# Shared access of VectorE and Pool counted as one queue in the planner, three places of a fused layer reordered

## The chip, the cores and the metric

The kernel runs on one core of a Trainium2 chip. The metric is the device time of one execution in microseconds (us). The engines are named as in the profile: PE (TensorE matmul, PEld its weight load), DVE (VectorE), ACT (ScalarE), POOL (GpSimd) and SP (SyncE, which issues all DMAs here). A matmul result lies in PSUM, which has eight banks; POOL instructions in this program never touch PSUM.

## What is computed

One layer over 1024 latent tokens and 256 context tokens, width 1024, in fp32 accuracy. Cut to what matters:

```python
pl = project(modulate(x, sh_x, sc_x), w_in)       # 11 streams out of one projection
pc = project(modulate(ctx, sh_c, sc_c), w_in)
s_f, s_b = final states of the context            # gated linear attention (GLA)
o_gla = bidir_gla(q, k, v, la_f, la_b, s_f, s_b)  # 4 heads, chunks of 64, two directions
q1, q2, k1, k2, dv = diff_streams(...)            # 8 heads: RMS norm, gains, rotary positions
...
a = softmax(s1) - lam * softmax(s2)               # differential attention over 1280 keys
o_diff = a @ v
a = rms_norm(o_gla) * gla_gain * silu(gla_gate)
b = rms_norm(o_diff) * diff_gain * silu(diff_gate)
y = sigmoid(m_gla) * (a @ w_br_gla) + sigmoid(m_diff) * (b @ w_br_diff)
return x + g_x * (y @ w_out)
```

## The kernel before

Every large product is made of three matmuls (`mm3`): an operand is split into a rounded high part `hi` and a rest `lo`, and hi·hi, hi·lo and lo·hi are added up in one PSUM bank. A split costs one copy that rounds (on ACT, or on POOL from SBUF) and one subtraction (on DVE or POOL).

Instructions of PE, ACT, DVE and POOL stand in the order in which a planner, `Driver` (L58), emits them. The program is a set of Python generators. Each yields the time at which it wants to go on; `Driver.op` (L96) keeps a clock of each engine (`free`), adds a cost to it for each instruction (given by `Engine.emit`, L189) and notes when a tile is ready, `LAT` after the end. The generator that is due earliest, by priority, emits next. On the chip each engine then works through its own list in that order and waits by semaphores. `either` (L374) takes DVE or POOL for a subtraction, by whose clock gives the earlier end.

The stages, in the order of time: the modulated input `h` (to about 100 us); the plain projection jobs of `stream` (L889), under which the first half of the GLA runs (`gla_a`, L1450: decays, factors, scores); then `sevens` (L1090), four projections (28 products instead of 32, in the manner of Strassen) whose input sums `sums7` (L925) makes on DVE, POOL and ACT out of `h` in tiles `p`, split into tiles `s7`. Its operand "s2" is written over half of `h`, which the plain jobs still read: `before` therefore stores the sum to DRAM (`d_s2`) and loads it back after the plain jobs. `weights7` (L988) loads and combines the weights for it (tiles `ra`, `rb`, `raw`, split into `w`). Next the last plain jobs (`second`: two tiles of gates, and the query projection `dq`), under which the second half of the GLA runs (`gla_b`, L1653; banks `gs`, `go`, `gt`). A `dq` tile goes through `post_qk` (L1367): ACT copies it to a tile `p` and squares it, DVE sums the squares, POOL raises them to -1/2 and scales the tile, then PE transposes it (`tp`) and the store `d_qT` follows.

Then attention: 64 units (8 heads by 8 query tiles). PE makes scores `s` in banks s0, s1, st; DVE takes maxima (`att_max`); ACT the exponentials `e5`; DVE mixes both (`att_mix`); PE transposes the result in 128-key blocks into one of two banks `b1` (`att_tr`, L1977), 4 + 4 + 2 blocks, where the two tails of a pair of units share one bank; `split2` (L2059) lets ACT copy the bank to a tile `ac` (two of them), and POOL rounds it and subtracts (`at`); PE multiplies with the values (`att_av`). Where attention leaves PE free, a filler runs, `fill` (L2135): the remaining gates, and the two branch products, half a tile (24 matmuls) at a time in a bank `mb`, held back by `pace`; what is left of it runs behind attention, in banks `mc`. Its weights `wt` are split by ACT and DVE (`conv`, L2153). Last comes the output projection.

Memory is handed on in pools that are opened and closed like a stack from the left or the right side (`POOLS`, L247). `mb` lies in pool `psW`, opened on the left by `to_b` when all plain jobs are through; the GLA's banks are pool `psA1`, on the right, closed by `to_gla` when the GLA is through (`ev_b2`).

Of the kernel before, what the change touches and what calls it, by code (L numbers as in the profile page):

```python
# [19 lines left out]
P = 128  # L20
# [36 lines left out]
class Driver:  # L57
# [9 lines left out]
    LAT = dict(PE=0.24, ACT=0.15, DVE=0.15, POOL=0.15)  # L67
# [3 lines left out]
    def __init__(self):  # L71
        self.now = 0.0
        self.free = dict(ACT=0.0, DVE=0.0, POOL=0.0, DGE=0.0, DMA=0.0)
        self.ready, self.last = {}, {}
        self.seq = 0
        self.due, self.future, self.blocked = [], [], 0
# [19 lines left out]
    def op(self, eng, cost, outs, ins):  # L96
# [3 lines left out]
        for x in ins:  # L100
            t = max(t, self.ready.get(self.key(x), 0.0))
# [4 lines left out]
        for x in outs:  # L106
            if eng != "PE":
                t = max(t, self.ready.get(self.key(x), 0.0))
        end = t + cost
        if eng == "PE":  # L110
            self.now = end
        else:
            self.free[eng] = end
# [4 lines left out]
        end += self.LAT[eng]  # L118
        for x in outs:
            self.ready[self.key(x)] = max(end, self.ready.get(self.key(x), 0.0))  # L120
        return At(end)
# [58 lines left out]
class Engine:  # L180
# [5 lines left out]
    def __getattr__(self, what):  # L186
        f = getattr(self.eng, what)

        def emit(out, *args, **kw):  # L189
# [23 lines left out]
            return self.d.op(self.name, c, outs, ins)  # L213
# [8 lines left out]
class Hybrid:  # L222
# [26 lines left out]
                 psA="left", psW="left", psB="left", psC="left", psA1="right", psB1="right", psD="right")  # L249
# [124 lines left out]
    def either(self, out, a, b, op):  # L374

        n = out.free_size()
        dve = self.d.free["DVE"] + 0.16 + 0.00104 * n <= self.d.free["POOL"] + 0.18 + 0.00216 * n
        return (self.dve if dve else self.pool).tensor_tensor(out, a, b, op)

    EDGE = 96  # L380


    def build(self):
        tc = self.tc
        with (
# [4 lines left out]
            with tc.manual_schedule(engines={ENG.PE, ENG.Activation, ENG.DVE, ENG.Pool}):  # L390
# [8 lines left out]
                self.close("psC", "psW", "psD", "sbW", "sbC", "sb", "sbE")  # L399
# [525 lines left out]
    def sums7(self):  # L925
# [7 lines left out]
        ev_s2 = [Event() for _ in range(4)]  # L933
        self.ev_op = {(o, k): Event() for o in self.ORDER[:7] for k in range(4)}
# [10 lines left out]
        for k in range(4):  # L945
# [13 lines left out]
            self.store([(self.d_s2[k], v["11"])], ev=ev_s2[k])  # L959
# [10 lines left out]
        for k in range(4):  # L970
# [17 lines left out]
    def weights7(self, groups):  # L988
# [96 lines left out]
        d.spawn(load(), prio=3)  # L1085
        d.spawn(sums(), prio=3)
        d.spawn(run(), prio=3)
# [119 lines left out]
    def to_gla(self):  # L1207
# [10 lines left out]
        self.open("sbW", "sbB2", "psB1")  # L1218
# [148 lines left out]
    def post_qk(self, isk, c, i, pm, tg):  # L1367
# [45 lines left out]
        e = self.pool.tensor_tensor(r, r, ss.unsqueeze(2).to_broadcast([P, 8, 64]), ALU.mult)  # L1413
# [640 lines left out]
    def att_split(self, g, pt, hi, lo, evs, tag):  # L2054
        e = yield from self.split2(pt, hi, lo, tag, g in self.SG)
# [3 lines left out]
    def split2(self, pt, hi, lo, tag, pool):  # L2059
# [13 lines left out]
        self.rel("ac", e)  # L2073
        return e
# [60 lines left out]
    def fill(self):  # L2135
# [32 lines left out]
        yield self.ev_b  # L2168
# [68 lines left out]
        while n < len(todo):  # L2237
# [8 lines left out]
            for half in range(2):  # L2246
                for x in two:
                    yield pace(i)
# [328 lines left out]
```

## Time and profile before

| what | value |
|---|---|
| three runs | 1728.13, 1728.68 and 1729.07 us, median 1728.68 |
| the profiled execution | 1727.89 us, its span 1726.2 us |
| mean granted TensorE clock | 0.986 of full |
| busy shares of the span | PE 95%, PEld 79%, DVE 68%, POOL 53%, ACT 47% |
| chain that ended last, by engine | PE 75%, POOL 9%, DVE 7%, issue 4%, ACT 3%, DMA 2% |
| DMA | 300.79 MB, mean 174 GB/s |

An execution is 1.7 us longer than its span. In the rows of the profile a line is mostly that of a helper (L190 for all DVE, ACT and POOL instructions, L329 for matmuls, L355 for transposes), so rows are told apart by tiles: `mm<-h,w` reads "tile mm, made from tiles h and w". A matmul's own duration is longer than its distance to the next one, since they overlap.

### The profile page before, as it was taken

What the parts mean: (1) busy time and instruction counts of PE and PEld (TensorE: products, weight loads), DVE (VectorE), ACT (ScalarE), POOL (GpSimd) and SP (SyncE); (2) the same over time, 40 slices, a digit from 0 to 9 for tenths busy, and PEclk for the clock granted to TensorE, in tenths of its full rate; (3) what the DMA queues carried; (4) which work ended last, traced back from release to release, by engine and by line L of the source; (5) the groups of instructions that cost most, each with busy time, mean ns of one, the idle gap of its engine ahead of it and who ended that gap; (6) DMA issues with size and microseconds to landing.
All of it is one profiled execution on the core that took longest, in us unless ns stands there. A gap on an engine that the chain in (4) does not pass through costs nothing.

```text
span 1726.2 us, 24883 instructions
## 1 busy us (share of the span) xinstructions
PE 1646.2 (95%) x8381; PEld 1362.3 (79%) x8381; DVE 1175.0 (68%) x1876; ACT 804.2 (47%) x1606; POOL 920.9 (53%) x908
## 2 busy tenths in 40 slices
PE   8899999999899999999999798999999998899999
PEld 3687788888788888888888587888878787787887
DVE  4764986875624366767686488788887887625694
ACT  4684655643332344343233366566665655511231
POOL 1500886785523245656566448788887888820000
PEclk9999999999999999999999899999999999999999
DMA  8636565544434474459999724335477434259421
GB/s 303 194 138 221 157 208 189 163 127 139 129 117 151 152 239 149 145 181 283 298 313 296 219 72 122 107 112 145 111 228 239 126 116 123 80 196 353 156 99 73
DMA packets 268688, 300.79 MB, mean 174 GB/s; under 512 B 23784, under 2 KB 186512, under 8 KB 268560
## 3 DMA queue, kind: packets, MB, share of 16 engines
q1 hardware_dynamic: 268560, 299.20, 55.5%
q8 instruction: 66, 1.08, 0.3%
q14 instruction: 62, 0.51, 0.1%
HBM read 197.94 MB, written 101.19 MB: 173 GB/s over the span
## 4 chain that ended last, share of the span: by engine, by line
PE 75%; POOL 9%; DVE 7%; issue 4%; ACT 3%; DMA 2%; SPq 0%; ACTq 0%; POOLq 0%; DVEq 0%
PE mm L329 21%; PE mc L329 10%; PE ma L329 10%; POOL at L190 6%; PE gs L329 5%; PE mb L329 5%; PE s L329 5%; PE b L329 4%; PE go L329 4%; PE gt L329 3%; PE tp L329 2%; DVE sm L190 2%; PE b L355 2%; PE tp L355 2%; DMA w<-in_w_ada 1%
## 5 line engine op out<-in xcount | busy, mean ns | idle before, releaser
L190 POOL TENSOR_TENSOR at<-ac,at 128x512 fp32r<-128x512 f32 x160 | 233.2, 1457 | 13.4
L190 DVE TENSOR_REDUCE sm<-s 128x1 f32<-128x1024 f32 (+1 forms) x192 | 197.5, 1040 | 42.5 <-PE s L329 38.4
L329 PE MATMUL mm<-w,h 128*128 128x512 f32 x864 | 219.2, 402 | 6.0 <-DVE us L190 6.0
L190 ACT ACTIVATE e<-s,sm 128x1280 f32<-128x1280 f32 x128 | 169.8, 1330 | 77.1 <-DVE sm L190 63.5
L329 PEld LDWEIGHTS mm<-w,h 128*128 128x128 f32 x864 | 162.1, 191 | 39.5 <-DVE us L190 6.6
L190 POOL TENSOR_SCALAR at<-ac 128x512 fp32r<-128x512 f32 x160 | 136.1, 851 | 95.2 <-ACT ac L190 90.0
L329 PE MATMUL s<-kk,aq 128*128 128x512 f32 (+1 forms) x768 | 174.7, 363 | 6.8 <-ACT e L190 6.1
L329 PE MATMUL mb<-h,wt 128*128 128x512 f32 x576 | 155.4, 404 | 4.5 <-DVE wt L190 3.1
L329 PE MATMUL mm<-h,w 128*128 128x512 f32 x576 | 149.1, 410 | 5.1 <-ACT w L190 3.2
L190 ACT ACTIVATE ac<-b 128x512 f32<-128x512 f32 x169 | 100.5, 598 | 109.8 <-PE b L355 67.4
L329 PEld LDWEIGHTS s<-kk,aq 128*128 128x128 f32 x768 | 122.5, 190 | 27.5 <-ACT e L190 10.7
L329 PE MATMUL b<-at,vv 128*128 128x256 f32 x960 | 128.6, 283 | 11.6 <-ACT ac L190 7.6
L329 PEld LDWEIGHTS mm<-h,w 128*128 128x128 f32 x576 | 111.1, 197 | 31.1 <-ACT w L190 3.9
L329 PE MATMUL mc<-h,wt 128*128 128x512 f32 x576 | 134.1, 393 | 0.8 <-DVE wt L190 0.5
L329 PEld LDWEIGHTS b<-at,vv 128*128 128x128 f32 x960 | 119.3, 188 | 18.5 <-ACT ac L190 9.9
L190 DVE TENSOR_TENSOR w<-raw,w 128x512 fp32r<-128x512 f32 x89 | 79.9, 920 | 73.5 <-ACT w L190 57.3
L329 PEld LDWEIGHTS mc<-h,wt 128*128 128x128 f32 x576 | 107.5, 188 | 25.1 <-DVE wt L190 1.0
L329 PEld LDWEIGHTS mb<-h,wt 128*128 128x128 f32 x576 | 102.1, 189 | 23.7 <-DVE wt L190 4.0
L190 DVE SCALAR_TENSOR_TENSOR e<-e,sm,e 128x1280 f32<-128x1280 f32 x64 | 115.7, 1808 | 1.1
L190 POOL TENSOR_TENSOR w<-raw,w 128x512 fp32r<-128x512 f32 x23 | 33.4, 1453 | 153.3 <-ACT w L190 121.5
L329 PE MATMUL ma<-w,h 128*128 128x512 f32 x384 | 100.8, 402 | 2.6 <-DVE w L190 1.8
L190 POOL TENSOR_TENSOR sm<-sm,nhalf 128x8 f32<-128x8 f32 (+3 forms) x78 | 97.7, 1252 | 10.5 <-DVE sm L190 5.3
(375 smaller groups left out, 3338.3 us busy)
## 6 DMA issues: line engine op xcount, KB each, us to landing
raw<-in_w_in SPq DMA_DIRECT2D x40, 512.0 KB, 4.4
rb<-in_w_in SPq DMA_DIRECT2D x64, 256.0 KB, 3.0
aq<-d_qT SPq DMA_DIRECT2D x128, 128.0 KB, 3.0
d_kT<-pl SPq DMA_DIRECT2D x40, 256.0 KB, 3.1
d_dv<-pl SPq DMA_DIRECT2D x40, 256.0 KB, 2.4
kk<-d_kT SPq DMA_DIRECT2D x32, 320.0 KB, 5.0
gv<-d_v SPq DMA_DIRECT2D x40, 256.0 KB, 4.7
vv<-d_dv SPq DMA_DIRECT2D x16, 640.0 KB, 6.3
```

Source lines behind the costliest of these rows:

```text
L190: self.ins = f(out, *args, **kw).ins
L329: self.ins = self.nc.tensor.matmul(out, lhsT, rhs, start=start, stop=stop, skip_group_check=more).ins
L355: self.nc.tensor.transpose(out, src, self.ident[:n, :n])
```

## The change

It has five parts. **Planner:** `LAT`, the time to readiness, is cut for ACT, DVE and POOL; an engine is free again a little before its instruction ends (`OVER`); and DVE instructions with two SBUF inputs (or copies within SBUF, or scans) and all POOL instructions over 16 elements share one list of busy stretches, `path`, where one waits for the other or pushes it back. `either` looks at that list and takes DVE unless POOL would end over 0.7 us earlier (`LEAN`); the last scaling in `post_qk` of an evacuated tile may go to either engine. **Tails:** the third transposed group goes by `dpath`: ACT rounds it out of PSUM, DVE subtracts out of PSUM; no `ac`, no POOL. **Input sum:** once the plain jobs are through, `sums7` splits s2 at once into its place, without DRAM. **Filler's bank:** `psW` lies on the right and is opened when the GLA's banks close; the filler starts at that event, and its first three half tiles aren't paced. **Small:** the last group of a plain job behind the sevens is one tile and not two; two generators of `weights7` get priority 0 instead of 3.

```diff
-    LAT = dict(PE=0.24, ACT=0.15, DVE=0.15, POOL=0.15)
+    LAT = dict(PE=0.24, ACT=0.07, DVE=0.07, POOL=0.1)
+    OVER = dict(ACT=0.11, DVE=0.085, POOL=0.035)
+    SAME = 0.035
...
+    def gap(self, t, cost):
+
+        for a, b in self.path:
+            if t + 0.08 < a:
+                break
+            t = max(t, b - 0.08)
+        return t
...
+        if shares:
+            t = self.gap(t, cost)
+            path, o = [(t + 0.08, t + cost - 0.08)], t + cost - 0.08
+            for a, b in self.path:
+                if b > self.now - 2.0:
+                    x = max(0.0, o - a) if a > t else 0.0
+                    path.append((a + x, b + x))
+                    o = max(o, b + x) if a > t else o
+            self.path = sorted(path)
...
-            return self.d.op(self.name, c, outs, ins)
+            pair = sum(1 for x in ins if x.space != PSUM and x.free_size() > 1)
+            shares = n > 16 and what != "memset" and (self.name == "POOL" or self.name == "DVE") and (self.name == "POOL" or
+                pair > 1 or "scan" in what or what in ("tensor_scalar", "tensor_copy") and not psum)
+            return self.d.op(self.name, c, outs, ins, shares)
...
-        dve = self.d.free["DVE"] + 0.16 + 0.00104 * n <= self.d.free["POOL"] + 0.18 + 0.00216 * n
+        t = [max(self.d.free[e], self.d.when(a, b)) for e in ("DVE", "POOL")]
+        c = 0.16 + 0.00104 * n, 0.18 + 0.00216 * n
+        if PSUM not in (a.space, b.space):
+            t = [self.d.gap(*x) for x in zip(t, c)]
+        dve = t[0] + c[0] <= t[1] + c[1] + self.LEAN
...
+    LEAN = 0.7
...
-        return self.job(wd, n, tiles, lambda i, k: [self.ev_h[k, 2 if i >= 8 else i // 4]], mms, post, "w")
+        return self.job(wd, n, tiles, lambda i, k: [self.ev_h[k, 2 if i >= 8 else i // 4]], mms, post, "w", last=1 if self.ev_us.t is not None else 2)
...
-            self.store([(self.d_s2[k], v["11"])], ev=ev_s2[k])
+            if self.ev_plain.t is not None:
+                yield d.when(v["11"])
+                hi, lo = self.op7["s2", k]
+                self.act.activation(hi, v["11"], AF.Copy)
+                e2 = self.either(lo, v["11"], hi.bitcast(F32), ALU.subtract)
+                d.set(self.ev_op["s2", k], e2)
...
+            else:
+                self.store([(self.d_s2[k], v["11"])], ev=ev_s2[k])
...
-        d.spawn(load(), prio=3)
+        d.spawn(load(), prio=0)
         d.spawn(sums(), prio=3)
-        d.spawn(run(), prio=3)
+        d.spawn(run(), prio=0)
...
-        self.open("sbW", "sbB2", "psB1")
+        self.open("sbW", "psW", "sbB2", "psB1")
...
-        e = self.pool.tensor_tensor(r, r, ss.unsqueeze(2).to_broadcast([P, 8, 64]), ALU.mult)
+        e = (self.either if own else self.pool.tensor_tensor)(r, r, ss.unsqueeze(2).to_broadcast([P, 8, 64]), ALU.mult)
...
-        e = yield from self.split2(pt, hi, lo, tag, g in self.SG)
+        e = yield from (self.dpath(pt, hi, lo, tag) if g == 2 else self.split2(pt, hi, lo, tag, g in self.SG))
...
+    def dpath(self, src, hi, lo, tag):
+        self.act.activation(hi, src, AF.Copy)
+        yield self.d.on("DVE", hi)
+        e = self.dve.tensor_tensor(lo, src, hi.bitcast(F32), ALU.subtract)
+        self.rel(tag, e)
+        return e
...
-        yield self.ev_b
+        yield self.ev_b2
...
-                    yield pace(i)
+                    if i >= 3:
+                        yield pace(i)
...
-            self.open("psW", "psB", "sbB")
+            self.open("psB", "sbB")
```

The first place is PE's list where the plain jobs end and attention begins. Before, the last two tiles of `dq` (banks mm and ma) end together, their two transposes follow, then the first scores, then the filler:

```order
L329 MATMUL ma_9205<-w_8401,h_201_834 128x512
L329 MATMUL ma_9205<-w_8402,h_201_834 128x512
L329 MATMUL ma_9205<-w_8401,h_202_835 128x512
L355 MATMUL tp_9353<-ident,p_9314 128x128 x4
L355 MATMUL tp_9364<-ident,p_9316 128x128 x4
L329 MATMUL s_1967_9386<-kk_7482,aq_9280 128x512 x4
L329 MATMUL s_1967_9386<-kk_7482,aq_9280 128x256 x2
L329 MATMUL s_1967_9386<-kk_7485,aq_9283 128x256 x2
L329 MATMUL s_1967_9386<-kk_7485,aq_9283 128x512 x4
L329 MATMUL mb_9410<-h_65_373,wt_9292 128x512
```

Now the last tile alone is in `ma`; the transpose of the tile before it (p_9247) follows, then the filler:

```order
L353 MATMUL ma_9246<-w_8229,h_201_831 128x512
L353 MATMUL ma_9246<-w_8230,h_201_831 128x512
L353 MATMUL ma_9246<-w_8229,h_202_832 128x512
L379 MATMUL tp_9326<-ident,p_9247 128x128 x4
L353 MATMUL mb_9352<-h_65_373,wt_9317 128x512
L353 MATMUL mb_9352<-h_66_374,wt_9317 128x512
L353 MATMUL mb_9352<-h_65_373,wt_9318 128x512
```

What moved: filler stands where nothing stood. 12 matmuls of `mb` lie between the last two transposes and 36 more between the last transpose and the first scores; over the whole program `mb` gets 624 matmuls instead of 576, and `mc` 528 instead of 576 from the same weights. ACT's list at the same place, where the filler's weights are split, stands so now:

```order
L211 ACTIVATE p_9247<-mm_9152 128x512
L211 ACTIVATE p_9254<-p_9247 128x512
L211 ACTIVATE p_9286<-ma_9246 128x512
L211 ACTIVATE p_9288<-p_9286 128x512
L211 ACTIVATE wt_9317<-raw_8207 128x1024
L211 ACTIVATE wt_9319<-raw_8355 128x1024
L211 ACTIVATE pl_9331<-tp_9326 128x512
```

Here the weights of the first filler tile (wt_9317) come behind the copies of the last `dq` tile; before, they stood ahead of the copies of the last two.

The second place is DVE's list where PE begins the sevens. `us` is a result tile to which DVE adds a bank `mm`, and by that frees the bank. Before, twelve rows up to the first one:

```order
L190 TENSOR_TENSOR p_4696<-p_4694,p_4696 128x512
L190 TENSOR_TENSOR p_4694<-p_4692,p_4694 128x512
L190 TENSOR_TENSOR p_4692<-p_4696,p_4692 128x512
L190 TENSOR_TENSOR raw_4391<-raw_4391,ra_4397 128x512
L190 TENSOR_TENSOR s_981_4733<-p_4696,s_980_4732 128x512
L190 TENSOR_TENSOR ra_4397<-rb_4686,raw_4391 128x512
L190 TENSOR_TENSOR s_985_4748<-p_4694,s_984_4747 128x512
L190 TENSOR_TENSOR raw_4391<-raw_4391,ra_4399 128x512
L190 TENSOR_TENSOR w_4767<-ra_4395,w_4766 128x512
L190 TENSOR_TENSOR ra_4399<-rb_4706,raw_4391 128x512
L190 TENSOR_TENSOR h_170_709<-p_4772,h_169_708 128x512
L190 TENSOR_TENSOR us_4614<-us_4614,mm_4779 128x512
```

All four blocks of input sums stood ahead of it. Now the third block is half done there, and the fourth begins ten rows behind it:

```order
L211 TENSOR_TENSOR p_4691<-p_4695,p_4691 128x512
L211 TENSOR_TENSOR raw_4491<-raw_4491,ra_4499 128x512
L211 TENSOR_TENSOR us_4529<-us_4529,mm_4728 128x512
L211 TENSOR_TENSOR h_181_757<-p_4691,h_180_756 128x512
L211 TENSOR_TENSOR p_4697<-p_4697,p_4691 128x512
L211 TENSOR_TENSOR s_980_4766<-p_4695,s_979_4765 128x512
```

What moved: the sums start later against PE (the last score product of the GLA's first half stands 54 matmuls ahead of the sevens, and stood 144 ahead of them), and the addition that frees the bank has moved ahead of the fourth block.

The third place is DVE's list in attention, where a tail (`at` from a bank `b`) now stands among the maxima and mixes:

```order
L211 TENSOR_SCALAR sm_9558<-sm_9558,sm_9557 128x1
L211 SCALAR_TENSOR_TENSOR e_2003_9566<-e_2006_9581,sm_9601,e_2003_9566 128x1280
L211 TENSOR_REDUCE sm_9559<-s_1966_9430 128x1
L211 TENSOR_SCALAR sm_9559<-sm_9559,sm_9557 128x1
L211 TENSOR_TENSOR at_1996_9530<-b_2018_9622,at_1995_9529 128x512
L211 TENSOR_REDUCE sm_9619<-s_1966_9430 128x1
```

There are 32 such rows, and POOL's list has lost 32 pairs of `at`. Over the program DVE's list grows from 1878 instructions to 2072, POOL's shrinks from 910 to 684; of POOL's 226, 64 are the tails, and most others are subtractions and products of the stages ahead of attention (`w`, `gqr`, `gqe`, `gkk`, `ge`).

More of the change, by code (lines that the diff above doesn't have):

```diff
@@ L73, in __init__ @@
         self.free = dict(ACT=0.0, DVE=0.0, POOL=0.0, DGE=0.0, DMA=0.0)
-        self.ready, self.last = {}, {}
+        self.ready, self.last, self.wrote = {}, {}, {}
         self.seq = 0
+        self.path = []
         self.due, self.future, self.blocked = [], [], 0
@@ L94, in on, with op @@
         return On(max([self.ready.get(self.key(x), 0.0) for x in tiles], default=0.0), eng)
-    def op(self, eng, cost, outs, ins):
+    def gap(self, t, cost):
[4 more added lines that the diff above has]
+        return t
+    def op(self, eng, cost, outs, ins, shares=False):
         t = self.now if eng == "PE" else self.free[eng]
         shared = list(outs) + [x for x in ins if x.space == PSUM]
-        for x in ins:
-            t = max(t, self.ready.get(self.key(x), 0.0))
+        for x in ins if eng == "PE" else ins + list(outs):
+            k = self.key(x)
+            end, by = self.wrote.get(k, (0.0, ""))
+            r = self.ready.get(k, 0.0)
+            t = max(t, end + self.SAME if by == eng and eng != "PE" and r <= end + self.LAT[eng] + 1e-6 else r)
         for x in shared:
@@ L105, in op @@
             t = max(t, end if by == eng else end + self.LAT[by])
-        for x in outs:
-            if eng != "PE":
-                t = max(t, self.ready.get(self.key(x), 0.0))
+        if shares:
[7 more added lines that the diff above has]
+            self.path = sorted(path)
         end = t + cost
@@ L112, in op @@
         else:
-            self.free[eng] = end
+            self.free[eng] = end - self.OVER[eng]
         for x in ins + list(outs):
@@ L117, in op @@
                 self.last[k] = (end, eng)
-        end += self.LAT[eng]
         for x in outs:
-            self.ready[self.key(x)] = max(end, self.ready.get(self.key(x), 0.0))
-        return At(end)
+            k = self.key(x)
+            self.wrote[k] = (end, eng)
+            self.ready[k] = max(end + self.LAT[eng], self.ready.get(k, 0.0))
+        return At(end + self.LAT[eng])
     def dma(self, nbytes, dst, src):
@@ L248 @@
                  sbA1="right", sbG="right", sbS="right", sbA2="right", sbW="right", sbB2="right",
-                 psA="left", psW="left", psB="left", psC="left", psA1="right", psB1="right", psD="right")
+                 psA="left", psW="right", psB="left", psC="left", psA1="right", psB1="right", psD="right")
     def __init__(self, tc, nc, a, out):
@@ L933, in sums7 @@
         ev_s2 = [Event() for _ in range(4)]
+        late = [True] * 4
         self.ev_op = {(o, k): Event() for o in self.ORDER[:7] for k in range(4)}
@@ L969, in sums7 @@
         yield self.ev_plain
-        for k in range(4):
+        for k in [k for k in range(4) if late[k]]:
             yield from self.acq("p")
```

4 lines of the change are left out of this document (3 added, 1 removed).

## Prediction

> **What bounds the kernel now.** I read the page first, then busy time by stage, then who PE waits for, and last the timelines around its longest gaps.
>
> ```profile
> span 1726.2 us, 24883 instructions
> PE 1646.2 (95%) x8381; PEld 1362.3 (79%) x8381; DVE 1175.0 (68%) x1876; ACT 804.2 (47%) x1606; POOL 920.9 (53%) x908
> ```
>
> PE is busy for 95% of the span, and the change leaves its number of matmuls alone (the built lists have 8061 PE instructions before and after). So all that can be won are PE's 80 us of idle time (1726.2 - 1646.2) and the slow stretches behind gaps. The same by stages; the columns are length, busy us of PE, PEld, DVE, ACT and POOL, granted clock, DMA share and GB/s:
>
> ```profile
> 150.00:431.00 281.00, 275.38 (x1397) 230.29 (x1397) 208.38 (x355) 145.51 (x382) 195.43 (x243) 0.98 0.57 173
> 431.00:480.00 49.00, 43.05 (x180) 35.05 (x179) 30.48 (x33) 15.95 (x29) 22.25 (x14) 0.93 0.44 137
> 480.00:800.00 320.00, 319.46 (x1403) 262.80 (x1402) 174.58 (x217) 124.94 (x214) 141.47 (x101) 1.00 0.53 168
> 960.00:1003.00 43.00, 30.21 (x136) 23.93 (x135) 24.75 (x38) 15.02 (x24) 18.78 (x18) 0.84 0.72 196
> 1003.00:1500.00 497.00, 464.76 (x2900) 400.67 (x2900) 405.09 (x698) 302.10 (x590) 394.28 (x345) 1.00 0.46 133
> 1500.00:1656.00 156.00, 155.24 (x724) 128.19 (x723) 82.28 (x133) 31.77 (x54) 22.43 (x23) 1.00 0.66 223
> ```
>
> Idle are 5.6 us in the plain jobs (150 to 431), 6.0 at the start of the sevens, 12.8 at the passage to attention (960 to 1003), and 32.2 within attention (1003 to 1500). In the sevens (480 to 800) and behind attention PE is full: work taken out of those stretches shortens the kernel by its whole length, 319.46 / 1403 = 0.228 us a matmul. The clock is under 1.00 just where there are gaps. The longest of PE's waits name the same places:
>
> ```profile
> PE tp L355 <- POOL p L190: 15.7, 3, 10.3
> PE b L355 <- ACT ac L190: 8.8, 13, 1.3
> PE b L329 <- ACT ac L190: 7.6, 7, 1.9
> PE s L329 <- ACT e L190: 6.1, 11, 1.5
> PE mm L329 <- DVE us L190: 6.0, 1, 6.0
> ```
>
> **The passage to attention.** PE, ACT, DVE and POOL there (start, us, rows; in brackets the idle time before):
>
> ```profile
> 970.96 0.84 PE L329 MATMUL ma<-w,h 128*128 128x512 f32 x3
> 982.13 1.12 PE L355 MATMUL tp<-ident,p 128*128 128x128 f32 x4 [10.32 <-POOL p L190]
> 985.25 1.12 PE L355 MATMUL tp<-ident,p 128*128 128x128 f32 x4 [2.00 <-POOL p L190]
> ...
> 959.47 0.60 ACT L190 ACTIVATE p<-mm 128x512 f32<-128x512 f32 x1
> 969.57 2.00 ACT L190 ACTIVATE wt<-raw 128x1024 fp32r<-128x1024 f32 x2
> 971.46 0.58 ACT L190 ACTIVATE p<-mm 128x512 f32<-128x512 f32 x1
> 971.94 0.60 ACT L190 ACTIVATE p<-ma 128x512 f32<-128x512 f32 x1
> ...
> 970.65 2.36 DVE L190 TENSOR_TENSOR wt<-raw,wt 128x1024 fp32r<-128x1024 f32 x2 [0.25 <-ACT wt L190]
> ...
> 966.85 1.04 POOL L190 TENSOR_TENSOR p<-p,sm 128x512 f32<-128x512 f32 x1
> 973.85 4.46 POOL L190 TENSOR_TENSOR p<-p,kk 128x256 f32<-128x256 f32 x4 [5.96 <-DVE sm L190]
> ```
>
> The last matmul ends at 971.80 and the last two transposes wait for the chains of two tiles, which share POOL: 12.3 us of PE. The change puts filler there, whose weights must be split first. In the new order of ACT that split stands behind the copies of the last tile. By the rows above: copy 0.15 us after PE's end (971.94), the square and then the weights about 0.5 each later, so `wt` starts at 1.1 and its first tile ends at 2.2 (half of 2.00, and a start-up); DVE's half takes 1.2 more (half of 2.36), but only the third matmul reads it. PE's order has the transpose of the tile before in front. That tile's chain took 8.4 us before (959.47 to 967.89), and starts 5.9 us ahead of PE's end (24 matmuls and a transpose lie between); with its last scaling allowed on DVE and POOL free of a second tile I take 5.5 to 8.4, so it is ready between -0.4 and 2.5. First gap: 2.7 us. Then 12 filler matmuls take 2.7 us, to 5.4 or so, and the last tile's chain, 5.5 to 8.4 long, ends 0 to 3 us later: second gap 1.5. Of 12.3 us remain 4.2; between 2.2 and 5.7 seem possible. **Gain 8.1 us**, from 6.6 to 10.1. The filler that fills it, 48 x 0.228 = 10.9 us, is taken from behind attention, where nothing hides it: that is how the gain reaches the end.
>
> Gaps cost more than their length, since the clock falls. I let that loss stand as it is (0.84 in this stage), as gaps remain. The Trainium skill, "TensorE: Matmul & The Clock Gate", section "What's actually happening", states that the clock is halved after an idle window of about 3.4 us; by it both new gaps would be too short, and some 2 us more would be won, an estimate from that page. The 5.95 us gap of the next fence did slow the clock, but no single row here shows what a gap of under 3 us does at this place.
>
> **The start of the sevens.**
>
> ```profile
> 447.41 5.60 PE L329 MATMUL mm<-w,h 128*128 128x512 f32 x24
> 458.96 8.19 PE L329 MATMUL mm<-w,h 128*128 128x512 f32 x24 [5.95 <-DVE us L190]
> ...
> 442.88 4.08 DVE L190 TENSOR_TENSOR p<-h,h 128x512 f32<-128x512 f32 x3
> 447.00 2.15 DVE L190 TENSOR_TENSOR p<-p,p 128x512 f32<-128x512 f32 x3
> 458.23 0.67 DVE L190 TENSOR_TENSOR us<-us,mm 128x512 f32<-128x512 f32 x1
> ```
>
> PE waits 5.95 us for the addition that frees its bank, and then runs 24 matmuls in 8.19 us instead of 5.60: 8.5 us in all. DVE came late because all four blocks of input sums stood ahead, three of them at 1.36 us each (4.08 / 3) beside POOL, against 0.72 (2.15 / 3). In the new order the addition stands ahead of the fourth block, but the blocks start later: 54 matmuls (12 us) ahead of the sevens instead of 144 (33 us). From DVE's first sevens weight (row 499 of its new list) to the addition (row 531) are 32 instructions, at 0.6 to 0.75 us 19 to 24 us; PE needs the bank 96 matmuls after the sevens begin, 21.9 us. That is on the edge. Then PE needs the fourth block of s2 and its weights at 32.8 + 2 us (144 and 9 matmuls), and DVE has 54 instructions to there, 32 to 40 us. I take half of the loss as saved: **4.3 us**, between 8.5 and -3 (the wait moves to s2 and grows). The DRAM round trip of s2 goes (8 DMAs); SP is not waited for here, so it counts nothing.
>
> **Attention.** The groups that carry it, and the spread of the tiles `at`:
>
> ```profile
> L190 POOL TENSOR_TENSOR at<-ac,at 128x512 fp32r<-128x512 f32 x160 | 233.2, 1457 | 13.4
> L190 POOL TENSOR_SCALAR at<-ac 128x512 fp32r<-128x512 f32 x160 | 136.1, 851 | 95.2 <-ACT ac L190 90.0
> ...
> L190 DVE TENSOR_TENSOR pl<-tp,pl 128x512 fp32r<-128x512 f32 x35 | 24.0, 687 | 33.2 <-ACT pl L190 28.4 <-DMA aq<-d_qT 4.7
> ...
> L190 DVE SCALAR_TENSOR_TENSOR e<-e,sm,e 128x1280 f32<-128x1280 f32 x64 | 115.7, 1808 | 1.1
> ...
> L190 POOL TENSOR_TENSOR at<-ac,at x152: 1263/1292/2575, 1001.9 to 1499.3; 128x512 fp32r<-128x512 f32 x152
> ...
> ACT ac L190 <- POOL at L190: 46.1, 32, 3.6
> ```
>
> The tails take 32 x (1.457 + 0.851) = 73.9 us from POOL, of 394.3 busy in 497: from 79% to 64%. DVE gets 32 x 0.69 = 22.0 us (the row `pl<-tp,pl` is the same instruction out of PSUM): from 82% to 86%. ACT does as many copies as before. POOL's instructions run to 2.575 us where 1.292 is the median, so it and DVE hinder each other, and less of POOL helps DVE a little. What does POOL hold up? ACT waited 46.1 us for it to free `ac`, and PE waited 16.4 us for `ac` (8.8 + 7.6) and 2.0 for `at`, more than half of its 32.2. I take 8 us of these 18 as saved. Against it stands that a tail keeps its bank `b1` until DVE has subtracted, and DVE may be in an instruction of up to 1.81 us: an exposed wait of 32 x (1.81 + 0.69 - 0.6) = 61 us at the very worst, if nothing planned beside it covered any; nothing, if PE's order does. My 8 us are net of some 3 of this. **Gain 8 us**, with ends of 24 (three quarters of the idle time) and -22 (DVE binds; see the rivals).
>
> **The rest.** Some 140 instructions of the plain jobs' stretch and the sevens go from POOL to DVE, for 512 columns about 0.7 us each on DVE against 1.45 on POOL (the rows `pl<-tp,pl` and `at<-ac,at` above). There DVE was busy for 208 of 281 us and POOL for 195; PE has 5.6 us of idle time to win and no slack to lose. I take 0, between +5 and -8. The Trainium skill, "Perfetto Trace Analysis", section "Optimizing Scalar/DVE Operations", speaks against this part: the two engines share a read port, so moving work between them might not help. With that, this part would add nothing to the sum, which is what I have taken, and the second rival has the same for the sevens and attention.
>
> **The sum.** 8.1 + 4.3 + 8 + 0 = 20.4 us off the profiled 1727.9: 1707.5. The median of the runs is 0.8 above that execution: 1708.
>
> **Rivals.**
> 1. POOL was the throttle of attention: its relief frees three quarters of the idle time there, 24 us instead of 8. For it: the 46.1 us above. Against it: POOL itself waited 90.0 us for `ac`, so it is not full. 1708 - 16 = 1692. Chance 0.17.
> 2. Only the passage pays. The shift between POOL and DVE is worth nothing, the sevens' wait moves to s2, attention's idle time changes its name from POOL to DVE. For it: DVE is at 82% and takes more. 1728.7 - 8 = 1721. Chance 0.23.
> 3. Slower: DVE becomes the bound of attention. The place is the tail's subtraction, behind maxima and mixes in DVE's list; the price is its whole 22.0 us; it decides where DVE, at 86%, has no idle time left at the moments when banks are asked for, because maxima, exponentials and mixes follow each other in a ring. 1728.7 - 8.1 + 22 = 1743. Chance 0.09.
> 4. The filler doesn't do what it is for: its weights come late (they are split in memory that the GLA gives back, perhaps behind its stores), and the gap at the passage stays with another name, while the rest does nothing: 1726 to 1729. Chance 0.06.
>
> The forecast has 0.45. **How the numbers follow.** A measurement of this kernel can tell about 0.2%, 3.5 us, from no change. The range from 1693 to 1726 holds the forecast, the second rival, half of the first and a part of the fourth; outside are half of the first, the third and some of the fourth, 2 in 10. Faster by over 3.5 us are the forecast, rivals 1 and 2: 0.85; slower 0.09; the same 0.06.
>
> **What would show it.** Passage: PE's gaps between the last `ma` and the first `s` sum to about 4 us with `mb` between them, and `mc<-h,wt` has 528 matmuls; wrong if PE waits for `wt` over 5 us. Sevens: the wait for `us` is under 2 us and no wait for `h` or `s` of its size replaces it. Attention: POOL's busy share near 64%, ACT's wait for POOL far below 46 us, PE's idle time near 24 us; wrong if `PE b <- DVE at` comes up with over 10 us. The plain jobs: PE's idle time near 6 us; wrong if DVE's `gd`, `gqr` or `w` hold up PE.

## The result, and the profile after

| kernel | runs | median | ratio to before |
|---|---|---|---|
| before | 5 | 1728.13 us | |
| the changed kernel | 5 | 1717.10 us | 0.9938, 95% interval 0.9921 to 0.9954 |

The change makes the kernel 11 us faster, where 20 were forecast (1708, range 1693 to 1726). The profiled execution took 1718.92 us. The head of its page, first the span, then busy time by engine:

```profile
span 1717.2 us, 24802 instructions
PE 1650.2 (96%) x8381; PEld 1362.1 (79%) x8381; DVE 1220.5 (71%) x2070; ACT 806.9 (47%) x1609; POOL 681.0 (40%) x682
```

The stages of the prediction, with the same columns (length, busy us of PE, PEld, DVE, ACT and POOL, granted clock, DMA share, GB/s):

```profile
150.00:431.00 281.00, 272.58 (x1383) 227.87 (x1382) 201.71 (x423) 144.26 (x381) 118.93 (x162) 0.98 0.53 166
431.00:480.00 49.00, 48.46 (x203) 39.18 (x202) 42.21 (x60) 19.95 (x36) 14.31 (x7) 0.95 0.31 99
480.00:800.00 320.00, 317.31 (x1383) 260.21 (x1382) 190.67 (x266) 122.42 (x209) 69.06 (x49) 0.99 0.53 170
960.00:1003.00 43.00, 33.93 (x150) 26.25 (x149) 22.64 (x33) 13.93 (x25) 13.15 (x12) 0.92 0.73 201
1003.00:1500.00 497.00, 475.32 (x2930) 408.49 (x2929) 429.30 (x738) 306.81 (x595) 337.74 (x289) 0.99 0.48 136
1500.00:1656.00 156.00, 154.65 (x716) 127.00 (x715) 92.23 (x149) 33.08 (x55) 15.27 (x16) 1.00 0.64 215
```

POOL lost 240 us of work. PE's idle time in attention fell from 32.2 to 21.7 us; in the plain jobs it rose from 5.6 to 8.4 and in the sevens from 0.5 to 2.7. The longest of PE's waits now:

```profile
PE s L353 <- ACT e L211: 12.1, 22, 2.3
PE tp L379 <- DVE p L211: 8.5, 4, 4.9
PE b L379 <- ACT ac L211: 4.5, 5, 1.9
PE tp L379 <- ACT p L211: 4.5, 2, 3.5
PE gs L353 <- POOL gkk L211: 3.1, 1, 3.1
PE gs L353 <- DVE w L211: 2.9, 1, 2.9
PE mb L353 <- DVE wt L211: 2.9, 1, 2.9
```

The waits for `ac` (16.4 us in two rows) are down to 4.5; PE waits for exponentials instead. A share of idle time does not say where the time went, since an emptied stretch may only move. For that I use the start times, in the trace, of a few matmuls that both kernels have (us):

| start of | before | after | difference |
|---|---|---|---|
| first product with `s7` | 483.31 | 477.01 | -6.30 |
| last plain matmul | 971.42 | 970.60 | -0.82 |
| first score | 986.02 | 991.73 | +5.71 |
| last score | 1489.52 | 1487.00 | -2.52 |
| end of the span | 1726.17 | 1717.20 | -8.97 |

From row to row: 6.3 us won up to the first product with `s7`, 5.5 lost in the sevens and in the plain jobs behind them; the passage to attention became 6.5 us **longer**; attention 8.2 shorter; the rest 6.5 shorter. The passage on PE (start, us, rows; in brackets the idle time before):

```profile
965.27 5.72 PE L353 MATMUL ma<-w,h 128*128 128x512 f32 x24
973.82 0.63 PE L379 MATMUL tp<-ident,p 128*128 128x128 f32 x4 [2.83 <-DVE p L211]
974.20 0.71 PE L353 MATMUL mb<-h,wt 128*128 128x512 f32 x2
977.79 4.44 PE L353 MATMUL mb<-h,wt 128*128 128x512 f32 x10 [2.88 <-DVE wt L211]
982.08 0.60 PE L379 MATMUL tp<-ident,p 128*128 128x128 f32 x4
982.43 3.01 PE L353 MATMUL mb<-h,wt 128*128 128x512 f32 x12
986.13 5.77 PE L353 MATMUL mb<-h,wt 128*128 128x512 f32 x24 [0.69 <-ACT ft L211]
991.73 2.48 PE L353 MATMUL s<-kk,aq 128*128 128x512 f32 x12
```

The gaps sum to 6.4 us (2.83 + 2.88 + 0.69), from 12.3. But 36 filler matmuls, some 9 us, stand between the last transpose and the first score, which all of attention waits for. The experiments ask what that costs, and what each other part is worth.

### The profile page after: what moved, and what is told of

Read it like the earlier page. It is cut to its first block, busy times and chain, and to the rows that moved or that the text cites. A ratio compares the mean times of both kernels' runs of the same rounds, so it can differ in the third digit from the quotient of the medians.

```text
span 1717.2 us, 24802 instructions
## 1 busy us (share of the span) xinstructions
PE 1650.2 (96%) x8381; PEld 1362.1 (79%) x8381; DVE 1220.5 (71%) x2070; ACT 806.9 (47%) x1609; POOL 681.0 (40%) x682
## 4 chain that ended last, share of the span: by engine, by line
PE 66%; DVE 16%; ACT 5%; DMA 4%; issue 4%; POOL 3%; SPq 0%; ACTq 0%; DVEq 0%; POOLq 0%
PE mm L353 17%; PE ma L353 9%; PE mc L353 8%; DVE sm L211 5%; PE gs L353 5%; PE s L353 5%; PE mb L353 5%; PE b L353 4%; PE go L353 4%; PE gt L353 3%; DVE e L211 3%; PE b L379 2%; ACT e L211 2%; PE tp L353 2%; PE tp L379 1%
## 5 line engine op out<-in xcount | busy, mean ns | idle before, releaser
L211 POOL TENSOR_TENSOR at<-ac,at 128x512 fp32r<-128x512 f32 x128 | 188.0, 1469 | 10.7
L353 PE MATMUL s<-kk,aq 128*128 128x512 f32 (+1 forms) x768 | 180.0, 369 | 12.5 <-ACT e L211 12.1
L353 PE MATMUL mb<-h,wt 128*128 128x512 f32 x624 | 172.2, 410 | 6.1 <-DVE wt L211 2.9
L211 POOL TENSOR_SCALAR at<-ac 128x512 fp32r<-128x512 f32 x128 | 112.8, 881 | 155.1 <-ACT ac L211 136.0
L353 PEld LDWEIGHTS mb<-h,wt 128*128 128x128 f32 x624 | 111.9, 192 | 26.2 <-DVE wt L211 3.3
L353 PE MATMUL mc<-h,wt 128*128 128x512 f32 x528 | 123.2, 393 | 1.4 <-DVE wt L211 0.9
L353 PEld LDWEIGHTS mc<-h,wt 128*128 128x128 f32 x528 | 98.5, 188 | 24.7 <-DVE wt L211 1.8
L211 ACT ACTIVATE ac<-b 128x512 f32<-128x512 f32 x137 | 81.5, 600 | 58.2 <-PE b L379 46.6
L353 PE MATMUL ma<-w,h 128*128 128x512 f32 x384 | 95.9, 395 | 0.4 <-DVE gp L211 0.4
L379 PE MATMUL b<-ident,e 128*128 128x128 f32 x604 | 88.9, 277 | 7.4 <-ACT ac L211 4.5
```

Of the source, the lines that this page charges most:

```text
L211: self.ins = f(out, *args, **kw).ins
L353: self.ins = self.nc.tensor.matmul(out, lhsT, rhs, start=start, stop=stop, skip_group_check=more).ins
L379: self.nc.tensor.transpose(out, src, self.ident[:n, :n])
```

## The experiments

Each was timed beside runs of the kernel before (their medians: 1726.8 us for e1 to e4, 1727.4 for e5 to e8, 1727.2 for e9 to e12). In the table, as in the one above, are starts in its trace (us); "behind" is the count of `mc<-h,wt`, filler left for behind attention. 0.001 of ratio is 1.7 us.

| kernel | median | ratio, interval | first `s7` | first score | last score | behind | span |
|---|---|---|---|---|---|---|---|
| changed kernel | 1717.10 | 0.9938, 0.9921 to 0.9954 | 477.0 | 991.7 | 1487.0 | 528 | 1717.2 |
| e1 without bank | 1712.37 | 0.9917, 0.9904 to 0.9930 | 477.7 | 983.4 | 1481.7 | 552 | 1710.7 |
| e2 without tails | 1723.38 | 0.9977, 0.9967 to 0.9987 | 476.6 | 990.9 | 1490.5 | 528 | 1720.8 |
| e3 old planner | 1712.15 | 0.9912, 0.9898 to 0.9925 | 481.4 | 993.5 | 1475.7 | 576 | 1708.9 |
| e4 s2 by DRAM | 1727.18 | 1.0003, 0.9991 to 1.0015 | 488.4 | 1002.2 | 1494.2 | 528 | 1725.1 |
| e5 before + bank | 1731.17 | 1.0020, 1.0011 to 1.0029 | 483.5 | 992.0 | 1495.9 | 576 | 1731.9 |
| e6 before + tails | 1703.54 | 0.9860, 0.9847 to 0.9873 | 482.8 | 985.9 | 1468.3 | 576 | 1702.5 |
| e7 old planner, no bank | 1701.71 | 0.9854, 0.9841 to 0.9867 | 482.0 | 983.6 | 1466.5 | 576 | 1700.1 |
| e8 LEAN 0 | 1723.24 | 0.9979, 0.9970 to 0.9987 | 479.0 | 993.2 | 1496.3 | 528 | 1720.2 |
| e9 new planner to passage | 1699.43 | 0.9838, 0.9824 to 0.9851 | 477.8 | 983.5 | 1466.0 | 576 | 1699.0 |
| e10 new planner to sevens | 1698.62 | 0.9833, 0.9820 to 0.9847 | 477.3 | 980.1 | 1463.2 | 576 | 1696.8 |
| e11 bank, 24 ahead | 1715.84 | 0.9933, 0.9920 to 0.9945 | 481.6 | 983.3 | 1476.3 | 576 | 1711.9 |
| e12 no shared list | 1726.94 | 1.0003, 0.9993 to 1.0013 | 477.7 | 981.6 | 1480.1 | 576 | 1725.1 |

### Undoing one part at a time (e1 to e4)

The theory after the two traces was: the passage pays 4 to 5 us, the tails 3 to 5, the planner nothing in sum, the input sum little. e1 takes the bank back:

```diff
-                 psA="left", psW="right", psB="left", psC="left", psA1="right", psB1="right", psD="right")
+                 psA="left", psW="left", psB="left", psC="left", psA1="right", psB1="right", psD="right")
...
-        self.open("sbW", "psW", "sbB2", "psB1")
+        self.open("sbW", "sbB2", "psB1")
...
-        yield self.ev_b2
+        yield self.ev_b
...
-                    if i >= 3:
-                        yield pace(i)
+                    yield pace(i)
...
-            self.open("psB", "sbB")
+            self.open("psW", "psB", "sbB")
```

> The changed kernel with the filler's bank taken back: psW opens on the left behind the plain jobs as before, the first three half tiles are paced again. PE's order is the same up to the passage to attention, so everything ahead of 965 us should agree to 0.5 us. Theory A (the passage pays what the two traces show, 11 us of filler taken from the end against 6.5 us of later start of attention): 4 to 5 us slower than the changed kernel, about 1721.5; mc<-h,wt has 576 matmuls again and PE's idle time between the last ma and the first s is over 10 us. Rival B (most of the passage's gain came from the planner's shorter chain of the last dq tile, which may now scale on DVE): less than 2 us slower, about 1718, idle time at the passage of 7 us or less. Rival C (filler early costs attention its own filler later, and the gain is only there where attention does not run dry): faster in attention by 3 us or more, sum within 1 us.

Not slower but 0.0021 faster, with intervals that overlap; so at least the gain that A promised isn't there. The first score came 8.3 us earlier. PE in the first head, with the bank (the changed kernel) and without (e1); columns as above:

```profile
991.70:1042.70 51.00, 45.73 (x265) 37.14 (x264) 42.32 (x67) 30.99 (x54) 24.03 (x21) 1.00 0.28 78
```

```profile
983.40:1034.30 50.90, 50.37 (x279) 42.44 (x280) 44.38 (x67) 30.61 (x50) 17.18 (x18) 0.97 0.50 129
```

The first head takes 51 us either way. Without the bank PE is full in it, since filler lies there; with the bank 48 matmuls of filler have gone ahead, 24 fewer lie in the first head, and PE is idle in it for 5.3 us instead of 0.5. That filler was moved from a place where it was free.

e2 splits the tails as before:

```diff
-        e = yield from (self.dpath(pt, hi, lo, tag) if g == 2 else self.split2(pt, hi, lo, tag, g in self.SG))
+        e = yield from self.split2(pt, hi, lo, tag, g in self.SG)
```

> The changed kernel with the tails split as before (ACT copies to ac, POOL rounds and subtracts). PE's order is the same up to the first units of attention. Theory A (POOL held up attention through ac, and VectorE took over as the bound at once, so that only a part came through): 3 to 5 us slower, about 1721, with ACT's wait for POOL at ac back above 30 us and POOL near 79% busy in attention. Rival B (the tails are worth nothing, attention gained by the planner's order): within 1.5 us, about 1717, the wait for ac comes back but PE's idle time in attention stays near 22 us. Rival C (tails cost: VectorE is the bound): 3 us or more faster, about 1714.

0.0039 slower, 6.7 us: more than A said. Of A's signs POOL's share came (80% in attention), but ACT's wait for POOL at `ac` was 13.6 us and not over 30; in the same stretch of the kernel before it is 41.6. In the changed kernel's order POOL holds up less than it did before.

e3 puts the planner's numbers back:

```diff
-    LAT = dict(PE=0.24, ACT=0.07, DVE=0.07, POOL=0.1)
-    OVER = dict(ACT=0.11, DVE=0.085, POOL=0.035)
+    LAT = dict(PE=0.24, ACT=0.15, DVE=0.15, POOL=0.15)
...
-            return self.d.op(self.name, c, outs, ins, shares)
+            return self.d.op(self.name, c, outs, ins)
...
-        dve = t[0] + c[0] <= t[1] + c[1] + self.LEAN
+        dve = self.d.free["DVE"] + 0.16 + 0.00104 * n <= self.d.free["POOL"] + 0.18 + 0.00216 * n
...
-        e = (self.either if own else self.pool.tensor_tensor)(r, r, ss.unsqueeze(2).to_broadcast([P, 8, 64]), ALU.mult)
+        e = self.pool.tensor_tensor(r, r, ss.unsqueeze(2).to_broadcast([P, 8, 64]), ALU.mult)
```

> The changed kernel with the planner's numbers of before (LAT, no OVER, no shared list, either by the clocks alone, last scaling on POOL); bank, tails, input sum and the small edits stay. Theory A (the planner gave 4.9 us in the plain jobs and took 5.5 us back in the sevens and the second plain jobs): the last plain matmul within 1.5 us of the changed kernel's 970.6, the sevens start near 431 and not 426; the end 1714 to 1721. Rival B (the planner is worth something by itself, in attention too): 1722 or more. Rival C (the planner is a net loss): under 1713.

0.0026 faster, by its time C: the planner is no gain here (the intervals overlap again). The sevens start at 428.8, between A's 426 and 431, and attention is 482.2 us long from first to last score instead of 495.3, though 72 filler matmuls ran ahead of it.

e4 takes the branch of the input sum away:

```diff
-            if self.ev_plain.t is not None:
+            if False:
```

> The changed kernel with s2 stored to DRAM and loaded back as before. PE's order is the same up to the GLA's scores shortly ahead of the sevens. Theory A (s2 in place puts ACT's and VectorE's splits ahead of the first weights of the sevens, and so makes the 2.9 us and 1.6 us waits for w there, while it saves nothing else): 0 to 3 us faster, 1714 to 1717, with the wait for w under 2 us. Rival B (s2 in place is what removed the wait for us): 2 to 4 us slower, about 1720, and a wait for us or s2 of over 4 us. Rival C: it does not matter, within 1 us.

11.2 us slower (0.0065), far more than any theory had. Around the place, in order of time:

```profile
464.70 0.32 SPq L318 DMA_DIRECT2D d_s<-p  x1
...
468.31 0.37 SPq L318 DMA_DIRECT2D p<-d_s  x1
...
472.27 0.63 ACT L211 ACTIVATE h<-p 128x512 fp32r<-128x512 f32 x1 [3.95 <-DMA p<-d_s]
...
472.95 1.65 PE L353 MATMUL gs<-w,h 128*128 128x512 f32 x3 [6.67 <-ACT h L211]
```

Since the new planner starts the sums late, the last block is stored at 464.70, loaded from 468.31 and split from 472.27, while PE wants it from 466: it waits 6.67 us. The branch is what lets the late start pay.

### One part alone, on the kernel before (e5, e6), and both undone (e7)

e5 adds to before the bank's lines, e6 the tails' (`dpath` and its call), e7 takes from the changed kernel the diffs of e1 and e3.

> The kernel before with the filler's bank alone. In the built order 72 filler matmuls (16.4 us at 0.2275 us each) now stand ahead of the first scores, and the weights that are left for behind attention are the same 576 matmuls as before; the 72 are missing in the first head. Theory A (what e1 and the changed kernel showed: the first head takes about 51 us however much filler lies in it, so the filler moved to the passage fills a place that was free and empties another that was free): first score 5 to 8 us later, first head 49 to 52 us with 5 us or more of PE idle in place of 0.5, the end within 3 us of the kernel before, ratio 0.998 to 1.002. Rival B (the prediction's step: the passage's gain reaches the end): 6.6 to 10 us faster, ratio 0.994 to 0.996.

3.5 us **slower**. 72 filler matmuls go ahead, the first score is 6.0 us later, and the span 5.7 longer; the first head takes 51.9 us with 7.1 us of PE idle; by the trace 35 of the 72 are missing in it, and the others in later heads. That is A, at the edge of its ratio, and the prediction's step falls.

> The kernel before with the tails' split alone. Same order up to the first units of attention. Theory A (the tails are worth 6 to 7 us wherever they are put, as the changed kernel without them lost): 5 to 8 us faster, ratio 0.995 to 0.997, ACT's wait for POOL at ac under 15 us, POOL near 68% in attention, and PE's waits in attention named e (exponentials) more than ac. Rival B (they pay only with the planner's order that gives VectorE's list room): within 2 us of before. Rival C (they pay more without the planner, since VectorE is less loaded by other work): 9 us or more faster, ratio under 0.995.

24 us faster, more than twice the whole change. By its size that is C; DVE is as busy as in the changed kernel, so C's reason is not borne out. Attention is 482.4 us from first to last score, from 503.5. Its stage, PE's wait for `ac`, and ACT's for POOL within 1003 to 1500 us:

```profile
1003.00:1500.00 497.00, 484.11 (x3050) 421.78 (x3048) 429.79 (x753) 309.40 (x609) 340.30 (x300) 1.00 0.48 138
```

```profile
PE b L355 <- ACT ac L190: 3.8, 7, 1.0
```

```profile
ACT ac L190 <- POOL at L190: 9.8, 9, 2.1
```

PE's idle time fell from 32.2 to 12.9 us with POOL at 68% and DVE at 86%, the same shares as in the changed kernel. In the kernel before ACT's wait for POOL in this stretch is 41.6 us. PE's waits for `ac` and for POOL's `at` fell there from 18.4 to 5.0 us, which is 13.4 of the 19.3 us of idle time that went. But with the tails the planner also orders attention anew, and e6 does not separate the two.

> The planner of before and the bank of before; tails, input sum and the small edits as in the changed kernel. Against e3 (the same with the bank) it gives the bank's worth under the old planner, against e6 that of the input sum and the small edits. Theory A (the bank is worth nothing or less, the planner costs 4 to 5 us): 1711 to 1715, ratio 0.991 to 0.993, like e3. Rival B (the bank pays under the old planner, whose passage was longer): 1718 to 1722, ratio 0.995 to 0.997.

9 us under A's range and 16 under B's: A's signs hold, its sizes don't. Against e3, which has the bank, e7 is 0.0058 or 10.0 us faster, and the first score is 9.9 us earlier. Against e6 it is the same within the intervals: input sum and small edits are worth nothing that can be seen under the old planner.

### Where the planner and the bank cost (e8 to e12)

e8 has `LEAN = 0.0`.

> The changed kernel with LEAN 0 in place of 0.7: the subtractions go to the engine that is planned to end first, so VectorE's list loses 77 instructions and POOL's gains 76. Theory A (the planner costs time in the sevens because VectorE is given too much: 61% busy and 22% POOL there, against 56% and 45% before): sevens main part 1 to 3 us shorter (first to last s7 product 277 to 279 us against 280.5), the end 2 to 5 us faster than the changed kernel, 1712 to 1715. Rival B (not the share of VectorE but the order of the lists costs it): within 1.5 us of the changed kernel. Rival C (less on VectorE brings back contention with POOL): 2 us or more slower, over 1719.

0.0041 slower, which is rival C's range, but no theory is tested by it: DVE's work in the sevens did not fall (191.2 us within 480 to 800, in the changed kernel 190.7). The sevens start 5.7 us earlier than in the changed kernel, and PE then waits for the last block of the input sum:

```profile
465.11 5.49 PE L353 MATMUL gs<-w,h 128*128 128x512 f32 x12 [9.46 <-ACT h L211]
```

From first to last score it takes 503.1 us, 7.8 more than the changed kernel; why, I have not traced.

In e9 a method `loose` puts LAT and OVER back (and takes out `SAME`, the planner's short step between two instructions of one engine), and a flag turns the shared list off, where attention begins; there is no bank. In e10 the same two lines stand at the end of the first loop of `sums7`.

```diff
+    def loose(self):
+
+        self.lat, self.over = dict(PE=0.24, ACT=0.15, DVE=0.15, POOL=0.15), dict(ACT=0.0, DVE=0.0, POOL=0.0)
+        self.tight = False
...
             d.set(self.ev_b)
+            d.loose()
+            d.share = False
```

> The changed kernel without the filler's bank, with the new planner up to the passage to attention and the old one (its LAT, no OVER, no shared list) from there on. In the built order each head has the same number of filler matmuls as in e7. Theory A (the planner's loss lies within attention, where its lists of VectorE, ACT and POOL interlock less well): ahead of the first score like e1 (983.4), from the first to the last score like e7 (482.9 us against 498.2 in e1), the end 1700 to 1704, ratio 0.984 to 0.987. Rival B (attention suffers from what the new planner leaves behind, such as late stores or a late start of an engine, not from its order): first to last score over 490 us, the end 1708 or more.

A on every point of the trace, with a time just under its range: first score as in e1, then 482.5 us of attention as in e7, and 0.0079, 13.6 us, faster than e1. First to last score in e9, and in e1, each with one wait of ACT in that stretch (line numbers shift with an edit):

```profile
983.50:1466.00 482.50, 469.54 (x2918) 407.26 (x2919) 424.92 (x735) 305.11 (x586) 321.02 (x283) 1.00 0.51 144
```

```profile
ACT e L217 <- DVE sm L217: 72.2, 39, 3.8
```

```profile
983.40:1481.70 498.30, 476.88 (x2930) 411.49 (x2931) 431.63 (x737) 304.39 (x584) 317.57 (x278) 0.99 0.51 141
```

```profile
ACT e L211 <- DVE sm L211: 89.5, 46, 4.8
```

Both have the same tails, and ACT and POOL have nearly the same work; what differs is the order, and 24 filler matmuls more in e1's attention (5.5 us). In e1 ACT waits 17 us more for the maxima, and PE is idle for 21.4 us, not 13.0.

> As e9, but the old planner takes over earlier, when the input sums of the sevens are all planned. Theory A (the new planner wins 4 to 5 us up to the first s7 product and gives them back between there and the last plain product, because VectorE gets too much): first s7 product near 477.5 as in e1, from there to the last plain product 489.5 us as in e7 (e1: 493.8), so the first score 3 to 4 us ahead of e7 and e9, the end 1696 to 1700, ratio 0.982 to 0.985. Rival B (what is won ahead of the sevens is only shifted, the later stage is bound by the input sums and comes out the same): the last plain product within 1 us of 971.6, the end like e9.

The fastest version, 1698.62 us, though not told apart from e9 (0.9833 and 0.9838). In the trace A holds: from the first product with `s7` to the last plain matmul (477.27 to 968.88) e10 takes 491.6 us, e9 493.9 and e7 489.7, so about half of what was lost there comes back. Against the changed kernel it is 18 us faster.

e11 is e7 with the bank, but all half tiles behind the first one are paced:

```diff
-                    if i >= 3:
-                        yield pace(i)
+                    if i >= 1:
+                        yield pace(i - 1)
```

> e7 with the filler's bank, but only the first half tile (24 matmuls) may go ahead of the first scores; in the built order it stands between the last two transposes, where PE is idle in e7, and no filler stands between the last transpose and the first scores. The filler left for behind attention is 576 matmuls as in e7. Theory A (the bank's cost is the delay of the first score by the filler in front of it, and attention keeps its own pace however much filler lies in it): first score within 2 us of e7's 983.6, the end within 3 us of e7, ratio 0.984 to 0.988. Rival B (PE bounds attention, so filler taken out of it shortens it): 4 to 6 us faster than e7, ratio 0.981 to 0.983. Rival C (it is the order that the bank makes in attention, not the delay): 1706 or more.

The passage on PE is as it should be, filler between the two transposes and the first score at 983.32, as without a bank:

```profile
973.54 1.11 PE L355 MATMUL tp<-ident,p 128*128 128x128 f32 x4 [3.06 <-POOL p L190]
974.31 6.92 PE L329 MATMUL mb<-h,wt 128*128 128x512 f32 x24
981.25 0.66 PE L355 MATMUL tp<-ident,p 128*128 128x128 f32 x4
```

And yet it is 13.6 us slower than e7: attention takes 493.0 us, with 30 filler matmuls fewer. A and B fall and C is left: with other places for the filler the planner makes another order of attention, and that one is slower. Which rows make it so, the run does not show; PE there waits 7.5 us for DVE's tails (7.0 and 0.5), in e7 2.3, so the cost to DVE that the prediction's third rival names does come up in this order.

e12 is e9 without `d.loose()`.

> As e9, but from the passage on only the shared list and the either that reads it are taken out; LAT and OVER stay new. Theory A (the shorter LAT and OVER make the lists too tight in attention, the shared list does no harm): first to last score 492 us or more, the end 1708 or more. Rival B (the shared list's pushed-back stretches make the order worse): like e9, first to last score 481 to 487 us, the end 1700 to 1704. The built order leaves 576 matmuls for behind attention in both.

A: 498.5 us from first to last score. LAT, OVER and `SAME`, without the shared list, are enough to make attention slow. What the shared list would do there alone wasn't run. Its span is 26 us longer than that of e9: 16 in attention and 12 behind the last score (27 more `mb` matmuls are left there, 6 us; the cause of the other 6 is open), less 2 ahead of the first.

## Why the prediction came out as it did

The time lay in its range, and most of its signs to be watched for came: `mc<-h,wt` 528, no long wait for `us`, ACT's wait for POOL 6.7 us in attention (41.6 before), PE waiting for DVE's tails 2.8 us. Its sum was 20.4 us, the profile shows 9.0. That the time lay in the range is in part luck: the first term came to nothing, and that of attention held only by errors that cancel. Term by term:

- **Passage, 8.1 predicted, nothing measured.** The gaps were 6.4 us and not 4.2, a small miss. What failed is the step "is taken from behind attention, where nothing hides it: that is how the gain reaches the end". Of the 48 matmuls that are missing there 24 are the planner's doing (e1 has 552 without the bank), and under the old planner the bank takes none away (e3, e5: 576). Counted over `mb` and `mc` together, 567 filler matmuls are left behind the last score in the changed kernel, 564 in e1 and 594 before, so the bank takes none away under the new planner either. The filler came out of attention, half of it out of the first head, which is 51 us long with or without it. And what stood behind the last transpose delayed the first score: e3 against e7, 9.9 us, 8.8 of which reach the end of the span. In the changed kernel the passage is 6.5 us longer, and the stretch behind the last score 6.5 shorter; that stretch is as short without the bank (229.0 us in e1, 230.2 in the changed kernel), so the 6.5 are not the bank's.
- **Sevens start, 4.3 predicted, 1.4 measured.** The first product with `s7` comes 6.3 us earlier, but 4.9 of them are won in the plain jobs ahead (the sevens begin at 426.20 and not at 431.09). The wait for `us` went (0.54 us are left). Two waits for weights, 1.6 and 2.9 us, took its place. "SP is not waited for here, so it counts nothing" was read from the order of before. With the sums started late, the trip through DRAM would have cost 11 us (e4); the in-place split is the costliest part to leave out.
- **The rest, 0 predicted:** 4.9 us won in those plain jobs, 5.5 lost between the first product with `s7` and the last plain matmul, 0.6 lost together. The zero was right as a sum, of two parts that the prediction did not have. e10 wins 2.3 of the 5.5 back (against e9) with the old planner there, under which POOL has 144.6 us of work within 480 to 800 and not 69.1. The shift does not pay in that stretch, as the second rival had it.
- **Attention, 8 predicted, 8.2 measured, by two errors that cancel.** The tails alone take 21.1 us out of it (e6, 503.5 to 482.4), the rest of the change puts 12.9 back. The first rival's size, 24 us, was right for the part, and its mechanism, POOL as the throttle, fits the waits that went. How much of the 24 is POOL's relief and how much the new order that came with it is not shown; in the changed kernel's order the tails are worth 6.7 us (e2). The argument that held the rival down, "POOL itself waited 90.0 us for `ac`, so it is not full", does not hold: in attention POOL waits even longer for `ac` in e6 (107.3 us, 73.7 before), and 24 us were won all the same. An engine with idle time can still be late at each moment when it is asked. The cost to DVE that the third rival feared is not seen in e6 (PE waits 2.1 us for DVE's tails); in e11 it is, at 7.5 us.
- **What the sum lacked.** It treated attention's order as a given. The lists are static, and with the same tails in them attention took from 482 to 503 us (e9, e8), depending on the planner's numbers and on where the filler starts. Cost of the new planner from the passage on: 13.6 us (e1 against e9). Cost of the bank: 10.0 us under the old planner (e3 against e7), with the new planner 3.6 (the changed kernel against e1, intervals overlapping). Which rows of the order do it is open; under the new planner ACT is seen to wait longer for DVE's maxima (e1 against e9), under e11 PE for DVE's tails.

The Trainium skill, "Perfetto Trace Analysis", section "Optimizing Scalar/DVE Operations", warns that moving work between DVE and POOL may not help since they share an SBUF read port. For the tails the runs differ: 24 us were won (e6), by the move together with the order that it brings. The moved subtraction has one operand in PSUM, and in e6 it was never stretched, while POOL was 68% busy (the row gives min, median and max in ns); that the PSUM operand is the reason was not tested:

```profile
L190 DVE TENSOR_TENSOR at<-b,at x30: 674/681/693, 1013.0 to 1466.0; 128x512 fp32r<-128x512 f32 x30
```

## What to carry to other kernels

Filler that is moved ahead pays only if it is then missing in a stretch that PE bounds, and only while it doesn't stand ahead of the instruction that the next stage starts with; count it in both places. It can also change the order of all that follows, as in e11, where attention became 10 us longer though its first score came no later. Time each part of a change to a planned order alone: here one part was worth 24 us, and two others took more than half of it back. New durations in a planner need not give a better order; where it is changed for one stage, keep it out of the others, or time each.

## What was not expected of the hardware

Gaps under 3 us can slow the clock. Behind two gaps of 2.88 us (that end at 429.59 and 977.79, both in the changed kernel) the windows show half the granted clock (the last number but two), and behind the second full clock again 4.5 us later:

```profile
977.70:982.20 4.50, 4.41 (x12) 3.44 (x13) 2.48 (x4) 0.00 (x0) 2.06 (x2) 0.53 1.02 282
982.20:986.00 3.80, 3.24 (x17) 2.38 (x15) 0.69 (x1) 1.75 (x3) 0.00 (x0) 1.00 1.20 290
...
429.50:434.60 5.10, 5.01 (x12) 3.95 (x13) 5.10 (x10) 1.29 (x3) 2.67 (x1) 0.50 0.45 145
```

Ten matmuls took 4.44 us there, and 12 took 3.01 right behind, so about 2 us were lost (4.44 - 10 x 0.2275 = 2.2). Neither gap stands alone: 2.83 us of idle time and 1.1 us of work lie ahead of the second, and the windows show half the clock from 975.07 on, when that gap had just begun. Ahead of the first lie 1.61 us of idle time and one matmul:

```profile
426.20 0.50 PE L353 MATMUL gs<-w,h 128*128 128x512 f32 x1 [1.61 <-ACT w L211]
429.59 5.06 PE L353 MATMUL gs<-w,h 128*128 128x512 f32 x11 [2.88 <-DVE w L211]
```

Nor does the length of a gap decide. At another place, where PE waits for `gb`, a gap of 1.95 us in the changed kernel was followed by half the clock, and one of 2.87 us in e2 by full clock (first the changed kernel, then e2):

```profile
701.51 5.75 PE L353 MATMUL mm<-w,h 128*128 128x512 f32 x17 [1.95 <-DVE gb L211]
702.00:705.40 3.40, 3.40 (x10) 2.63 (x9) 2.42 (x3) 0.63 (x1) 2.04 (x2) 0.50 0.16 60
...
702.40 4.83 PE L353 MATMUL mm<-w,h 128*128 128x512 f32 x20 [2.87 <-DVE gb L211]
702.40:707.00 4.60, 4.60 (x20) 3.83 (x21) 3.71 (x5) 1.33 (x3) 2.58 (x2) 1.00 0.15 57
```

What decides it is not shown by these runs. The prediction cited the Trainium skill, "TensorE: Matmul & The Clock Gate", section "What's actually happening", by which the gaps at the passage would be too short to halve the clock; the trace does not bear that out, and the 2 us that would have been won by it were not.
